# A decoder block in one kernel: attention operands laid out contiguously in DRAM, and the second supertile's SwiGLU operands kept there unsplit

## Chip, cores and metric

The kernel runs on one core of a Trainium2 chip. The metric is the device time of one execution in microseconds; the median of three timed executions before the change is 2718.97 us. The engines are named as in the profile: PE (matrix products), PEld (its weight loads), DVE (vector), ACT (scalar), POOL, and SP, whose queue issues every DMA of this kernel.

## What is computed

One layer on x of 2048 rows by 1024 columns, float32, with one final norm (`h` is RMSNorm(x)):

```
p = h @ W_in                                  # 1024 -> 2560 columns, split among three groups
a = pool_mixer(p[pool cols])                  # trailing means, 64x64 maps, 256 channels
b = diff_attention(p[diff cols])              # 4 heads: (softmax(q1 k1) - lam softmax(q2 k2)) v, causal
c = stick_breaking_attention(p[sb cols])      # 4 heads of 64
x = x + concat(a, b, c) @ W_out
x = x + (silu(h2 @ W_gate) * (h2 @ W_up)) @ W_down     # h2 = RMSNorm(x), 2816 inner columns
out = RMSNorm(x)
```

## The kernel before

All products are made of float32 parts that PE takes at its fast rate: an operand is **split** into a high part (a CAST on ACT, L415) and a low part (a subtraction on DVE, L416), and a product of two split operands is three matmuls (`mm3`, L474, L475, L476).

The program is one list of operations. A planner in the kernel (`Plan.schedule`) gives each operation a cost in ns, lets each engine take, in the order of a priority number, what it believes ready, and issues everything in the order of the planned starts. So every engine, and SP too, runs a fixed row of instructions, each waiting in its place until its inputs are there. The planner believes that a DMA of n bytes takes

```
def dma_ns(nbytes):
    return max(nbytes / 360.0, 450.0)
LAG = {..., "dma": (950.0, 950.0)}
MORE = {"dma": 1080.0, "pe": 0.0}
```

one after the other, and that its data can be read 950 + 1080 ns after that. SBUF is handed out by rings: a ring has some slots, and a new buffer waits until the oldest user of a slot is done.

**First half of the program: projections, attention, output projection.** The sequence is cut into four tiles of 512 rows. `a1_tile` normalizes a tile, multiplies with W_in and stores q, k and v, already split, in DRAM (stores at L611 for q and k, L595 for v). Attention then goes tile by tile over six pairs of heads (four differential, two stick-breaking). For each pair and tile, `load_q` brings q with 64 of its values on the partitions, twice, so that the high and low parts of k can stand under each other: buffer `q0` holds q's high part and `q1` its low part, each by two DMAs of 64 partitions (L626). `load_kv` brings k by two such DMAs (high part to partitions 0 to 63, low part to 64 to 127, L635) and v by one DMA of 128 partitions (L640) or two (L645). `scores` multiplies `q0` (L657) and then `q1` (L658) with k, for 128 query rows `g` at a time; every group of four `g` needs all of `q0` and `q1`. The work of `a1_tile` for the next tile has a lower priority and fills PE between the scores.

**Second half: SwiGLU.** The 2048 rows are two supertiles of 1024. A product of 2x2 blocks is done with seven block products (Strassen-Winograd): operand blocks 11, 21, 22 and sums T1 to T4, each cut in four pieces (`kk`), so 28 split operands. `gate_up` goes over 22 blocks `f` of weights; each takes seven products in four PSUM banks X, Y, W, Z. Some banks hold a partial sum that ACT copies out (L1118) or DVE adds up (L1122) before PE adds the next product to the same bank. The first two and the last two blocks of a supertile are interleaved in pairs.

While the first supertile's blocks run, `head_out` prepares the second supertile's operands in 16 side steps, one per block: eight `rows` steps (load x, norm, transpose on PE, store in `h_d`, L1057) and eight `operands` steps (load four pieces of `h_d`, L1064; four subtractions on POOL, L1070; four splits, L415 and L416; eight stores of the parts in `h1_d`, L1080). `head_in` then loads the 28 split operands (L1098, L1103) as their slots come free at the end of the first supertile. The buffers of the side steps come from a ring `x` of three slots; transposes take banks from the same ring `b` of eight banks as the products.

## Time and profile before

| | |
|---|---|
| timed executions | 2718.97, 2724.35, 2711.99 us |
| median | 2718.97 us |
| profiled execution: its own time | 2719.03 us |
| profiled execution: span from first to last instruction | 2717.2 us |
| PE, DVE, ACT, POOL busy | 96%, 66%, 49%, 32% of the span |
| mean granted TensorE clock | 0.977 |

The busy times are those of instructions in the profile. A matmul there lasts longer than the distance to the next one, since matmuls are pipelined; so idle time of PE is read from its waits and the granted clock, not from the busy share. Attention and the projections fill the span up to about 1383 us. The operand steps of the side work lie between 1576 us (first load at L1064) and 1716 us (last store at L1080); the second supertile's split operands are loaded from 1800 to 1853 us (L1098, L1103), around the change of supertiles; the last sums of gate and up (L1122) are at 2267 us, and the down products follow. The trace leaves the numbers out of names, so `h_d` in it stands for `h_d` and for `h1_d`.

### The profile page before, as it was taken

How to read it: one execution, taken by the hardware profiler on the slowest of the kernel's cores; microseconds unless marked ns; L12 is line 12 of the kernel's file. 1: busy time of each engine (PE TensorE's matmuls, PEld its weight loads, DVE VectorE, ACT ScalarE, POOL GpSimd, SP SyncE). 2: the span in 40 equal slices, each digit the busy share in tenths (PEclk: the TensorE clock that was granted, in tenths of full speed). 3: DMA queues.
4: the chain of work that ended last, by engine and by line, in shares of the span. 5: the costliest groups of instructions: out<-in, count | busy, mean ns of one | idle time of the engine just before them, and what ended most of it. 6: DMA issues, size and time to landing. Idle time of an engine off the chain costs nothing.

```text
span 2717.2 us, 39503 instructions
## 1 busy us (share of the span) xinstructions
PE 2601.9 (96%) x13836; PEld 2176.7 (80%) x13836; DVE 1786.2 (66%) x3131; ACT 1319.3 (49%) x2645; POOL 870.0 (32%) x890
## 2 busy tenths in 40 slices
PE   9989989989999999999989999999999998999998
PEld 7878778877888788888978877888888886888886
DVE  6366787758887888788656666545444447558557
ACT  4365566646666666665534444323333333445444
POOL 1001212212254124133015456535454544132041
PEclk9989999989999999999999999999999999999999
DMA  6786585556564775664534457465222338335223
GB/s 217 245 251 184 160 245 160 155 155 202 153 177 147 225 203 147 192 178 161 166 118 155 155 184 239 158 220 199 101 102 97 109 129 291 118 95 194 93 90 120
DMA packets 223480, 454.27 MB, mean 167 GB/s; under 512 B 23720, under 2 KB 70952, under 8 KB 223280
## 3 DMA queue, kind: packets, MB, share of 16 engines
q1 hardware_dynamic: 223280, 451.75, 52.9%
q8 instruction: 108, 1.77, 0.3%
q14 instruction: 92, 0.75, 0.1%
HBM read 321.11 MB, written 130.55 MB: 166 GB/s over the span
## 4 chain that ended last, share of the span: by engine, by line
PE 72%; DMA 9%; DVE 9%; issue 3%; ACT 2%; POOL 1%; SPq 1%; DVEq 0%; ACTq 0%; POOLq 0%
PE bank L474 16%; PE bank L476 16%; PE bank L475 16%; DVE d L416 4%; DMA d<-q_d 4%; PE bank L657 3%; PE bank L681 3%; PE bank L658 3%; DMA d<-wo_d 2%; PE bank L924 2%; PE bank L923 2%; PE bank L925 2%; ACT d L415 1%; PE bank L562 1%; PE bank L781 1%
## 5 line engine op out<-in xcount | busy, mean ns | idle before, releaser
L474 PE MATMUL bank<-d 128*128 128x512 f32 x2296 | 919.0, 400 | 14.0 <-DVE d L1122 9.8
L476 PE MATMUL bank<-d 128*128 128x512 f32 x2296 | 910.3, 396 | 5.7 <-DVE d L416 5.4
L416 DVE TENSOR_TENSOR d<-d 128x512 fp32r<-128x512 f32 (+2 forms) x672 | 614.6, 938 | 457.5 <-ACT d L415 281.2
L475 PE MATMUL bank<-d 128*128 128x512 f32 x2296 | 909.3, 396 | 3.4 <-DVE d L416 3.4
L415 ACT CAST d<-d 128x512 fp32r<-128x512 f32 (+2 forms) x672 | 489.0, 758 | 651.0 <-PE bank L476 352.3
L961 POOL TENSOR_TENSOR d<-d 128x512 f32<-128x512 f32 x336 | 520.0, 1556 | 846.3 <-DVE d L416 622.9
L474 PEld LDWEIGHTS bank<-d 128*128 128x128 f32 x2296 | 435.7, 190 | 116.0 <-DVE d L1122 12.4
L476 PEld LDWEIGHTS bank<-d 128*128 128x128 f32 x2296 | 434.3, 189 | 110.3 <-DVE d L416 8.7
L475 PEld LDWEIGHTS bank<-d 128*128 128x128 f32 x2296 | 434.8, 189 | 101.3 <-DVE d L416 5.1
L416 DVE TENSOR_TENSOR d<-bank,d 128x512 fp32r<-128x512 f32 (+3 forms) x381 | 219.3, 603 | 139.7 <-ACT d L415 138.7
L819 POOL TENSOR_TENSOR d<-d 128x512 f32<-128x512 f32 (+3 forms) x160 | 160.4, 1003 | 397.9 <-DVE d L815 375.6
L415 ACT CAST d<-bank 128x512 fp32r<-128x512 f32 (+3 forms) x381 | 187.5, 529 | 194.0 <-PE bank L681 122.0
L729 ACT ACTIVATE d<-bank,d 128x512 f32<-128x512 f32 (+3 forms) x320 | 198.9, 627 | 128.4 <-DVE d L726 120.3
L751 POOL TENSOR_SCALAR d<-d 128x512 f32<-128x512 f32 (+3 forms) x144 | 95.8, 681 | 448.7 <-ACT d L741 318.1
L726 DVE TENSOR_REDUCE d<-bank 128x1 f32<-128x512 f32 (+3 forms) x320 | 186.9, 602 | 61.6 <-PE bank L658 31.1
L657 PE MATMUL bank<-d 128*128 128x512 f32 (+3 forms) x480 | 203.7, 425 | 24.8 <-ACT d L729 9.0
L658 PE MATMUL bank<-d 128*128 128x512 f32 (+3 forms) x480 | 181.9, 382 | 25.5 <-DMA d<-q_d 25.5
L1122 DVE TENSOR_TENSOR d<-bank,d 128x512 f32<-128x512 f32 x176 | 121.0, 687 | 116.0 <-PE bank L476 98.7
L815 DVE TENSOR_TENSOR_SCAN d<-d,bank 128x512 f32<-128x512 f32 (+3 forms) x160 | 174.3, 1090 | 19.6 <-ACT d L807 8.1
L1118 ACT COPY d<-bank 128x512 f32<-128x512 f32 x132 | 77.3, 586 | 221.7 <-PE bank L476 196.9
L681 PE MATMUL bank<-ident,d 128*128 128x128 f32 x1088 | 157.5, 279 | 3.4 <-DVE d L772 2.6
L923 PE MATMUL bank<-d 128*128 128x256 f32 x512 | 149.5, 292 | 2.8 <-DMA d<-wo_d 1.1
(133 smaller groups left out, 3593.5 us busy)
## 6 DMA issues: line engine op xcount, KB each, us to landing
d<-in_w_gu_dram SPq DMA_DIRECT2D x88, 512.0 KB, 3.5
d<-in_w_in_dram SPq DMA_DIRECT2D x80, 512.0 KB, 4.6
d<-k_d SPq DMA_DIRECT2D x120, 256.0 KB, 6.6
d<-wo_d SPq DMA_DIRECT2D x52, 512.0 KB, 6.0
d<-q_d SPq DMA_DIRECT2D x96, 256.0 KB, 6.3
d<-vd_d SPq DMA_DIRECT2D x40, 512.0 KB, 4.9
g_d<-d SPq DMA_DIRECT2D x66, 256.0 KB, 2.1
d<-g_d SPq DMA_DIRECT2D x66, 256.0 KB, 2.7
```

Source lines behind the costliest of these rows:

```text
L415: pl.op("act", act_ns(n, psum), lambda: nc.scalar.copy(hi(), src()), r=r, w=[whi], prio=prio)
L416: pl.op("dve", dve_ns(n), lambda: nc.vector.tensor_sub(lo(), src(), f32(hi())), r=[*r, *after, whi], w=[wlo], prio=prio)
L474: nc.tensor.matmul(o, a_hi, b_hi, start=first, stop=False, **kw)
L475: nc.tensor.matmul(o, a_hi, b_lo, start=False, stop=False, **kw)
L476: nc.tensor.matmul(o, a_lo, b_hi, start=False, stop=last, **kw)
L657: nc.tensor.matmul(s.t[:, :n], q[0].t[:, r, qs], kt.t[:, r, :n], start=True, stop=False)
L658: nc.tensor.matmul(s.t[:, :n], q[1].t[:, r, qs], kt.t[:, r, :n], start=False, stop=j < t)
L681: nc.tensor.transpose(tp.t[:, c:c + P], rows[qb][kb // 4].t[:, (kb % 4) * P:(kb % 4 + 1) * P], ident)
L726: pl.op("dve", dve_ns(n), lambda s=s, n=n, mc=mc, sm=sm: nc.vector.tensor_reduce(sm.t[:, mc:mc + 1], s.t[:, :n], AX, ALU.max, negate=True) ...
L729: pl.op("act", act_ns(n, True, 2), lambda s=s, n=n, e=e, mc=mc, lc=lc, sm=sm: nc.scalar.activation(e.t[:, :n], s.t[:, :n], AF.Exp, bias=sm ...
L923: nc.tensor.matmul(o, m[:, 0, cs], wh.t[:, k % 4, :], start=k == 0, stop=False)
L961: pl.op(eng, ns, lambda: en.tensor_tensor(out(), a(), b(), op), r=r, w=w, prio=prio)
```

## The change

Five edits: the tensors in DRAM for q, k, v have one tile per pair and row tile, in the order in which attention reads them; q comes in two halves of 256 query rows (high and low part together), each one DMA whose partitions are the 64 values of q, each one twice; k comes by one DMA, with high and low part on alternating partitions, and v by one DMA; the transposes of the second half have banks 6 and 7 for themselves and the gate and up products banks 0 to 5; and `operands` stores T1 to T4 unsplit (`t_d`), while `head_in` loads them and the pieces of `h_d` and splits them there. The side steps get a rising priority number instead of one for all.

```diff
-    q_d = [dram.tile([2, P, S], F32, name=f"q_d{p}") for p in range(PAIRS)]
-    k_d = [dram.tile([2, P, S], F32, name=f"k_d{p}") for p in range(PAIRS)]
-    vd_d = [dram.tile([P, S // P, 2, P], F32, name=f"vd_d{p}") for p in range(DIFF_PAIRS)]
-    vs_d = [dram.tile([P, S // P, 2, 64], F32, name=f"vs_d{p}") for p in range(2 * SB_PAIRS)]
+    q_d = [[dram.tile([2, 64, 2, 2, 256], F32, name=f"q_d{p}_{t}") for t in range(NT)] for p in range(PAIRS)]
+    k_d = [[dram.tile([64, 2, 2, TQ], F32, name=f"k_d{p}_{t}") for t in range(NT)] for p in range(PAIRS)]
+    v_d = [[dram.tile([P, D], F32, name=f"v_d{p}_{t}") for t in range(NT)] for p in range(PAIRS)]
...
-                    pl.op("dma", dma_ns(P * 4096), lambda st=st, dst=dst[pair]: nc.sync.dma_start(
-                        dst[:, :, t0:t0 + TQ].rearrange("l p t -> p l t"), f32(st.t)),
-                        r=[st], w=[mk[pair][t]], prio=prio)
+                    for r in range(2):
+                        pl.op("dma", dma_ns(P * 2048), lambda st=st, dst=dst[pair][t], r=r, isq=isq: nc.sync.dma_start(
+                            dst[:, :, r].rearrange("h d l t -> d h (l t)") if isq else dst[:, :, r],
+                            f32(st.t[64 * r:64 * r + 64])), r=[st], w=[(mk[pair][t], r)], prio=prio)
...
     def load_q(pl, rg, t, p, prio):
-        q = [rg["q0"].new(), rg["q1"].new()]
-        for hl in range(2):
-            for dup in range(2):
-                pl.op("dma", dma_ns(64 * 4096) * 1.3, lambda hl=hl, dup=dup: nc.sync.dma_start(
-                    f32(q[hl].t[64 * dup:64 * dup + 64]),
-                    q_d[p][hl, :, t * TQ:(t + 1) * TQ].rearrange("(r d) t -> d r t", r=2)),
-                    r=[m_q[p][t]], w=[(q[hl], dup)], prio=prio)
+        q = []
+        for h in range(2):
+            qh = rg["q"].new()
+            q.append(qh)
+            pl.op("dma", dma_ns(P * 4096), lambda h=h, qh=qh: nc.sync.dma_start(
+                f32(qh.t), q_d[p][t][h].rearrange("(d o) r l t -> d o (r l t)", o=1).to_broadcast([64, 2, D])),
+                r=[m_q[p][t]], w=[qh], prio=prio)
...
-        for hl in range(2):
-            pl.op("dma", dma_ns(64 * 4096) * 1.3, lambda hl=hl: nc.sync.dma_start(
-                f32(k.t[64 * hl:64 * hl + 64]),
-                k_d[p][hl, :, j * TQ:(j + 1) * TQ].rearrange("(r d) t -> d r t", r=2)),
-                r=[m_k[p][j]], w=[(k, hl)], prio=prio)
...
+        pl.op("dma", dma_ns(P * 4096), lambda: nc.sync.dma_start(
+            f32(k.t), k_d[p][j].rearrange("d l r t -> (d l) r t")), r=[m_k[p][j]], w=[k], prio=prio)
+        pl.op("dma", dma_ns(P * 4096), lambda: nc.sync.dma_start(f32(v.t), v_d[p][j]), r=[m_v[p][j]], w=[v], prio=prio)
...
-            nc.tensor.matmul(s.t[:, :n], q[0].t[:, r, qs], kt.t[:, r, :n], start=True, stop=False)
-            nc.tensor.matmul(s.t[:, :n], q[1].t[:, r, qs], kt.t[:, r, :n], start=False, stop=j < t)
+            nc.tensor.matmul(s.t[:, :n], qh.t[:, c0:c0 + P], kt.t[:, r, :n], start=True, stop=False)
+            nc.tensor.matmul(s.t[:, :n], qh.t[:, c0 + 256:c0 + 256 + P], kt.t[:, r, :n], start=False, stop=j < t)
...
-                        pt = rg["b"].new()
+                        pt = rg["bt"].new()
...
-                for src, i, n, n0 in ((raw, 1, 2, 0), (raw, 3, 1, 2), (tt, 0, 2, 3), (tt, 2, 2, 5)):
-                    o = rg["x"].new([2, 2, 256], F32R)
-                    flat = lambda v, n=n: v.rearrange("p n t -> p (n t)")
-                    split(pl, lambda o=o, n=n: flat(o.t[:, 0, :n, :]), lambda o=o, n=n: flat(o.t[:, 1, :n, :]),
-                          lambda src=src, i=i, n=n: flat(src.t[:, i:i + n, :]), n * 256, False,
-                          [(src, i + m) for m in range(n)], (o, 0), (o, 1), prio)
-                    for l in range(2):
-                        pl.op("dma", dma_ns(P * 1024 * n), lambda o=o, l=l, n=n, n0=n0: nc.sync.dma_start(
-                            h1_d[kk][:, n0:n0 + n, l, c * 256:(c + 1) * 256], f32(o.t[:, l, :n, :])),
-                            r=[(o, l)], w=[(m_h1[kk], (n0, l, c))], prio=prio)
+                pl.op("dma", dma_ns(P * 4096), lambda: nc.sync.dma_start(
+                    t_d[kk][:, :, c * 256:(c + 1) * 256], tt.t), r=[tt], w=[(m_t[kk], c)], prio=prio)
...
-            return [lambda b=b: rows(b) for b in range(8)] + [
-                lambda kk=kk, c=c: operands(kk, c) for kk in range(4) for c in range(2)]
+            return [lambda b=b: rows(b, prio + b) for b in range(8)] + [
+                lambda kk=kk, c=c: operands(kk, c, prio + 8 + 2 * kk + c) for kk in range(4) for c in range(2)]
...
-                for kk in range(4):
+                for k2 in (0, 2):
+                    raw = rg["x"].new([2, TQ], F32)
+                    if n[0] == "T":
+                        for i in range(2):
+                            load(pl, (raw, i), lambda raw=raw, i=i: raw.t[:, i, :], t_d[k2 + i][:, int(n[1]) - 1, :],
+                                 [m_t[k2 + i]], P * 2048, prio)
                     else:
...
+                        k, c0 = k2 + 4 * (n[0] == "2"), TQ * (n[1] == "2")
+                        load(pl, raw, lambda raw=raw: raw.t, h_d[k:k + 2, :, c0:c0 + TQ].rearrange("k p t -> p k t"),
+                             [m_h], P * 4096, prio)
+                    for i in range(2):
+                        kk = k2 + i
...
+                        split(pl, hi, lo, lambda raw=raw, i=i: raw.t[:, i, :], TQ, False, [(raw, i)], kh, kl, prio)
+                        ops[n][kk] = (hi, lo, kh, kl)
...
-        q0=ring([2, TQ], F32R, ("w", [31, 12])), q1=ring([2, TQ], F32R, ("w", [32, 13])),
+        q=ring([D], F32R, ("w", [31, 32, 12, 13])),
...
-        b=banks(range(8)),
+        b=banks(range(6)), bt=banks((6, 7)),
     )
+    rm["bd"] = banks(range(8))
```

The whole kernel now issues 1264 DMAs instead of 1419. Because the costs and buffers that the planner sees are others, it plans the whole program anew, so the order on every engine changes from the first attention pair on. Three places follow; a name `d_` with a number is a buffer in SBUF, and lines of the changed kernel have other numbers.

SP's row where the q of one pair of the third tile is stored and loaded, before (`L611` is the store, `L626` the loads, `L640` loads of v, `L412` loads of weights, `L707` a store of attention's output):

```order
L611 DMA q_d2_62<-d_6060 128x2x512
L626 DMA d_6113<-q_d2_62 64x2x512
L412 DMA d_6123<-in_w_in_dram 128x1024
L626 DMA d_6113<-q_d2_62 64x2x512
L611 DMA q_d3_63<-d_6118 128x2x512
L412 DMA d_6166<-in_w_in_dram 128x1024
L626 DMA d_6181<-q_d2_62 64x2x512 x2
L640 DMA d_6201<-vd_d2_74 128x1024
L707 DMA o_d2_82<-d_6214 128x512
```

The same place now (`L613` the stores, `L630` the loads of q's halves, `L637` of k, `L639` of v):

```order
L637 DMA d_6054<-k_d2_1_93 128x1024
L613 DMA q_d2_2_70<-d_6076 64x2x512 x2
L630 DMA d_6137<-q_d2_2_70 128x1x1024
L412 DMA d_6153<-in_w_in_dram 128x1024
L630 DMA d_6170<-q_d2_2_70 128x1x1024
L613 DMA q_d3_2_74<-d_6142 64x2x512 x2
L412 DMA d_6199<-in_w_in_dram 128x1024
L639 DMA d_6218<-v_d2_1_117 128x1024
L698 DMA o_d2_134<-d_6258 128x512
```

Four loads of 64 partitions have become two of 128, the first of which is enough for the first scores, and the store has become two of 64 partitions. In the whole row of SP, 14 loads of q or k stand within six places behind the store that they read.

DVE's row at an operand step of the first supertile, before (`L1122` adds a bank to a buffer, `L416` is a split's low part, `L1128` a product):

```order
L416 TENSOR_TENSOR d_17593<-d_17559,d_17593 128x512
L1122 TENSOR_TENSOR d_17599<-bank3_170,d_17599 128x512
L416 TENSOR_TENSOR d_17619<-d_17425,d_17572 128x1024
L416 TENSOR_TENSOR d_17632<-d_17559,d_17632 128x256
L416 TENSOR_TENSOR d_17642<-d_17588,d_17642 128x512
L416 TENSOR_TENSOR d_17664<-d_17588,d_17664 128x512
L416 TENSOR_TENSOR d_17679<-d_17525,d_17621 128x1024
L1122 TENSOR_TENSOR d_17689<-bank7_186,d_17677 128x512
L1122 TENSOR_TENSOR d_17677<-bank5_178,d_17677 128x512
```

The same stretch now:

```order
L1111 TENSOR_TENSOR d_17509<-bank2_218,d_17509 128x512
L416 TENSOR_TENSOR d_17532<-d_17345,d_17487 128x1024
L416 TENSOR_TENSOR d_17592<-d_17443,d_17534 128x1024
L1111 TENSOR_TENSOR d_17599<-bank1_214,d_17590 128x512
L1111 TENSOR_TENSOR d_17590<-bank0_210,d_17590 128x512
```

The four splits of the side step (512, 256, 512, 512 columns) are gone from between the additions of banks, which are now at `L1111`.

ACT's row in the first supertile's last two blocks, before (`L1118` copies a bank, `L1125` is silu, `L415` a split's high part):

```order
L1118 COPY d_18610<-bank0_158 128x512
L1118 COPY d_18631<-bank1_162 128x512
L415 CAST d_18652<-d_18580 128x1024
L1125 ACTIVATE d_18610<-d_18610 128x512
L415 CAST d_18676<-d_18605 128x1024
L1125 ACTIVATE d_18631<-d_18631 128x512
L1118 COPY d_18701<-bank0_158 128x512
L1118 COPY d_18723<-bank1_162 128x512
```

The same place now, with `L1107` for the copies (`d_18477`, `d_18489` and `d_18541` are loads from `h_d` and `t_d`):

```order
L1107 COPY d_18463<-bank4_226 128x512
L415 CAST d_18486<-d_18404 128x1024
L415 CAST d_18513<-d_18477 128x512
L415 CAST d_18534<-d_18477 128x512
L1107 COPY d_18546<-bank3_222 128x512
L415 CAST d_18554<-d_18489 128x512
L415 CAST d_18560<-d_18489 128x512
L415 CAST d_18568<-d_18541 128x512
L1107 COPY d_18575<-bank4_226 128x512
L415 CAST d_18577<-d_18541 128x512
```

The splits that left the side steps now stand between the copies of the last two blocks, and each waits there for its load.

## Rows read from the trace of the kernel before

**Rows 1.** The page, parts 1 and 2: busy time of PE; PE's granted clock.

```profile
PE 2601.9 (96%) x13836; PEld 2176.7 (80%) x13836; DVE 1786.2 (66%) x3131; ACT 1319.3 (49%) x2645; POOL 870.0 (32%) x890
...
PEclk9989999989999999999999999999999999999999
```

**Rows 2.** Windows: length, busy us (instructions) of PE, PEld, DVE, ACT, POOL; PEclk; DMA.

```profile
0.00:1383.00 1383.00, 1298.00 (x8241) 1128.31 (x8241) 1015.43 (x1969) 804.35 (x1801) 325.54 (x526) 0.96 0.63 186
1383.00:1600.00 217.00, 214.93 (x948) 174.28 (x949) 137.06 (x208) 96.44 (x179) 92.86 (x64) 0.98 0.40 138
1600.00:1700.00 100.00, 90.96 (x374) 71.55 (x373) 67.76 (x71) 41.45 (x65) 66.13 (x51) 0.97 0.70 235
1700.00:1800.00 100.00, 99.82 (x431) 80.61 (x430) 50.24 (x57) 35.04 (x51) 47.52 (x33) 1.00 0.38 129
1800.00:1880.00 80.00, 80.00 (x347) 64.87 (x346) 39.62 (x41) 26.47 (x37) 35.53 (x25) 1.00 0.79 286
```

**Rows 3.** PE's waits in the whole span: total us, times, longest us.

```profile
PE bank L658 <- DMA d<-q_d: 25.5, 14, 3.7
PE bank L474 <- DVE d L1122: 9.8, 6, 3.7
PE bank L657 <- ACT d L729: 9.0, 13, 2.8
PE bank L657 <- DMA d<-k_d: 6.5, 3, 3.4
...
PE bank L657 <- DMA d<-q_d: 2.0, 3, 1.3
```

**Rows 4.** Timeline of PE at 576 to 583 us: start, length, instruction, [idle before <- releaser].

```profile
576.30 0.45 PE L657 MATMUL bank<-d 128*128 128x512 f32 x1
...
580.45 0.77 PE L658 MATMUL bank<-d 128*128 128x512 f32 x1 [3.70 <-DMA d<-q_d]
```

**Rows 5.** Timeline of SP's queue at 570 to 590 us.

```profile
571.09 1.24 SPq L626 DMA_DIRECT2D d<-q_d  x2
```

**Rows 6.** The page, part 6: DMA issues, KB each, median us from issue to landing.

```profile
d<-k_d SPq DMA_DIRECT2D x120, 256.0 KB, 6.6
...
d<-q_d SPq DMA_DIRECT2D x96, 256.0 KB, 6.3
d<-vd_d SPq DMA_DIRECT2D x40, 512.0 KB, 4.9
...
q_d<-d SPq DMA_DIRECT2D x24, 512.0 KB, 3.4
k_d<-d SPq DMA_DIRECT2D x24, 512.0 KB, 4.9
```

**Rows 7.** Instructions of L626 and of L640: ns min/median/max that SP is busy.

```profile
L626 SPq DMA_DIRECT2D d<-q_d x96: 573/580/1285, 38.3 to 1149.7; - x96
...
L640 SPq DMA_DIRECT2D d<-vd_d x40: 319/326/1323, 63.3 to 1152.8; - x40
```

**Rows 8.** Waits of SP's queue in the whole span.

```profile
SPq L635 <- DMA k_d<-d: 17.8, 8, 3.6
```

**Rows 9.** Waits of all engines from 1600 to 1700 us.

```profile
ACT d L415 <- DMA h_d<-d: 23.5, 11, 4.7
...
ACT d L415 <- DMA d<-h_d: 19.2, 6, 5.7
...
PE bank L474 <- DVE d L1122: 8.5, 4, 3.7
```

**Rows 10.** Timeline from 1622 to 1632 us.

```profile
1624.60 0.62 ACT L415 CAST d<-d 128x512 fp32r<-128x512 f32 x1 [5.67 <-DMA d<-h_d]
...
1628.54 0.50 PE L474 MATMUL bank<-d 128*128 128x512 f32 x1 [3.73 <-DVE d L1122]
```

**Rows 11.** Groups by form, 1600 to 1720 us: busy, mean ns | idle before.

```profile
L416 DVE TENSOR_TENSOR d<-d 128x512 fp32r<-128x512 f32 x28 | 27.4, 981 | 26.0 <-ACT d L415 26.0
...
L415 ACT CAST d<-d 128x512 fp32r<-128x512 f32 x28 | 17.4, 620 | 43.6 <-DMA d<-h_d 20.8 <-DMA h_d<-d 8.7 <-PE bank L476 8.7
```

More of the change, by code (lines that the diff above doesn't have):

```diff
@@ L310, in hybrid_block_kernel @@
     h_d = dram.tile([KB, P, 2 * TQ], F32, name="h_d")
-    h1_d = [dram.tile([P, 7, 2, TQ], F32, name=f"h1_d{k}") for k in range(4)]
+    t_d = [dram.tile([P, 4, TQ], F32, name=f"t_d{k}") for k in range(4)]
     ident = const.tile([P, P], F32, name="ident")
@@ L399, in hybrid_block_kernel @@
     m_g = [{n: [Buf() for _ in range(NH)] for n in GNAMES} for _ in range(2)]
-    m_h, m_h1 = Buf(), [Buf() for _ in range(4)]
+    m_h, m_t = Buf(), [Buf() for _ in range(4)]
     m_va = [Buf() for _ in range(NT)]
@@ L545, in a1_tile @@
         if t == 0:
-            constants(pl, {"w": rb["q1"], "h": rb["p0"]}, prio + 0.5, xs[3:])
+            constants(pl, {"w": rb["q"], "h": rb["p0"]}, prio + 0.5, xs[3:])
         late = []
@@ L1036, in head_out, with rows @@
         def head_out(prio):
-            def rows(b):
+            def rows(b, prio):
                 xb = rg["x"].new()
@@ L1043, in rows @@
                 for k4 in range(2):
-                    pt = rg["b"].new()
+                    pt = rg["bt"].new()
                     def tr(k4=k4, pt=pt):
@@ L1058, in rows, with operands @@
                     h_d[:, :, b * P:(b + 1) * P].rearrange("k p t -> p k t"), ht.t), r=[ht], w=[(m_h, b)], prio=prio)
-            def operands(kk, c):
+            def operands(kk, c, prio):
                 raw, tt = rg["x"].new([4, 256], F32), rg["x"].new([4, 256], F32)
@@ L1090, in head_in @@
             for n in ("11", "21", "T2", "T1", "T3", "T4", "22"):
[L1091 to L1105 removed]
+                for k2 in (0, 2):
[4 more added lines that the diff above has]
+                                 [m_t[k2 + i]], P * 2048, prio)
+                    else:
+                        k, c0 = k2 + 4 * (n[0] == "2"), TQ * (n[1] == "2")
[3 more added lines that the diff above has]
+                        kk = k2 + i
+                        if spare[0] and n[0] != "T" or n == "T4" and kk == 3 and spare[0]:
+                            spare[0] -= 1
+                            kh, kl = rg["hh"].new(), rg["hl"].new()
+                            hi, lo = (lambda kh=kh: kh.t), (lambda kl=kl: kl.t)
+                        else:
+                            h = rg["hw"].new()
+                            hi, lo, kh, kl = (lambda h=h: h.t[:, 0, :]), (lambda h=h: h.t[:, 1, :]), (h, 0), (h, 1)
+                        split(pl, hi, lo, lambda raw=raw, i=i: raw.t[:, i, :], TQ, False, [(raw, i)], kh, kl, prio)
+                        ops[n][kk] = (hi, lo, kh, kl)
@@ L1317, in down @@
                 four = range(4)
-                new = lambda: [rg["b"].new() for _ in four]
+                new = lambda: [rg["bd"].new() for _ in four]
                 X = new()
```

44 lines of the change are left out of this document (11 added, 33 removed).

## The prediction, made before the changed kernel was run

> **What bounds the kernel now.** I read the page first. PE is busy for 96% of the span, no other engine for more than 66% [rows 1], so a change pays only where it takes away idle time of PE or lets the granted clock stay up. The windows say where that is [rows 2]: up to 1383 us PE is idle for 1383 − 1298 = 85 us, and the mean granted clock is 0.96. [...]
>
> PE's waits name the causes [rows 3]. The largest is L658, the second product of a score, for loads of q: 25.5 us in 14 waits, with 2.0 us more at L657. Loads of k cost 6.5 us. The 9.8 us of L474 behind DVE's L1122 belong to the second half; 8.5 of them lie between 1600 and 1700 us [rows 9]. The long waits of the first half are followed by a slow clock: after the wait at 580.45 us the matmul lasts 0.77 us, where the one before it lasted 0.45 [rows 4].
>
> **Loads of q (edit 1).** At 576.30 us L657 runs, since `q0` has landed, and L658 then stands until 580.45 us for `q1` [rows 4], whose two loads SP issued from 571.09 to 572.33 us [rows 5]. One load of q occupies SP for 0.58 us and lands 6.3 us after its issue (medians) [rows 6, 7]. The fourth one therefore lands 3 × 0.58 + 6.3 = 8.0 us after the first is issued. The planner counts 4 × 0.95 + 2.03 = 5.8 us for it, by the constants in the code, so L658 stands in PE's row 2.2 us too early; the measured waits average 27.5 / 17 = 1.6 us.
> Now the first scores need one load, of 512 KB to 128 partitions. The trace has that shape in the load of v: 0.33 us on SP, 4.9 us to landing [rows 6, 7]. The planner counts 1.46 + 2.03 = 3.5 us, so the products stand 1.4 us too early. Loads that arrive 3.1 us sooner thus give only 0.8 us per wait, because the planner moves the products up by the other 2.3. Scaled, the 27.5 us become 27.5 × 1.4 / 2.2 = 17.5 (saved: 10); taking 0.8 off each of 17 waits saves 14. I take 12. Ends: 0, if PE waits as before, and 27.5.
>
> **Loads of k (edit 2).** By the same reckoning the second half of k landed 0.6 + 6.6 = 7.2 us after the first issue [rows 6], against 3.9 planned; now 4.9 against 3.5. The 6.5 us shrink by (3.3 − 1.4) / 3.3: saved, 4. Ends 0 and 6.5. Loads of v are fewer by 20; no wait of PE for v stands among the rows, so that is worth nothing by itself.
>
> **Stores of q and k (edit 3).** Each of 48 stores becomes two of 64 partitions. The 128-partition store lands after 3.4 (q) to 4.9 us (k) [rows 6]; no row shows a store of 64 partitions. From below, the second half goes out 0.37 us later and lands as the whole did; from above, it takes as long as the 64-partition loads, 6.3 us, so up to 0.4 + 2.9 = 3.3 us more. SP already stood 17.8 us in 8 waits for a k just being stored [rows 8], and everything behind such a wait on SP's queue stands too: weights, v, the next q. In the new order 14 loads follow their store closely. Ends: 14 × 0.4 = 6 and 14 × 3.3 = 46 us. I take 6, since each half carries half of the bytes.
> [...]
>
> **Clock.** In the first half 55 us of clock loss stand beside 85 us of idle time, 0.65 per us. Net idle time saved there is 12 + 4 − 6 = 10 us, so the clock gives back another 6.
>
> **The operand steps (edit 4).** Between 1600 and 1700 us ACT's casts wait 23.5 us for their buffers' stores and 19.2 us for loads of `h_d` [rows 9]. In one case ACT stands 5.67 us for such a load, its cast is late, DVE's subtraction behind it too, and so is L1122, for whose bank PE then waits 3.73 us [rows 10]. The change takes all casts, subtractions and part stores out of these steps; loads, POOL's subtractions and one store stay. What goes is the 9.0 us of idle time in that window and 0.03 × 100 = 3 us of clock [rows 2]: saved, 12 us. The count agrees: 57 matmuls at 100 / 431 = 0.232 us are 13 us. Ends: 0, if POOL's wait for the same loads delays its weight sums instead, and 13.
>
> **Splits at the change of supertiles (edit 5).** The 28 splits now run around 1800 to 1880 us: 28 × 0.98 = 27 us on DVE and 28 × 0.62 = 17 us on ACT [rows 11]. DVE is busy there for 39.6 us of 80 and ACT for 26.5 [rows 2], so 67 and 44 of 80: they fit, and the cover is that idle time. But each now stands in the queue behind a load, and copies of banks stand behind them. Since the last two blocks are interleaved, between a product and the next one in the same bank lie three others, 36 matmuls or 8.4 us at 0.232; waits for a load of the size of [rows 10] fit into that once. I take 2 us. Ends: 0, and 14 loaded pairs of operands at 12 / 8 = 1.5 us (what a side step costs now): 21.
>
> **At nothing:** six banks for the products instead of eight, and graded priorities. A block holds four banks at a time, and from 1383 to 1600 us, with all transposes of the side steps, PE idles for 2 us of 217 [rows 2]. If that cover is gone, transposes and copies stand in PE's way as in the operand steps, some 1 us per step: 8 us.
>
> **Sum,** against the profiled execution's own 2719.0 us (0.1 over the median): −12 − 4 + 6 − 6 − 12 + 2 = −26, that is 2693 us.
>
> **Rivals.**
> *A: the waits for q move to the first product.* PE's row is planned anew, and where q has only just been computed the products move up as far as the loads get faster. For it: 27.5 us in 17 waits look like a planner's error, and that error stays. Then the first half gives nothing, the second −10: 2709.
> *B: the half stores (slower).* Place: SP's queue behind the 14 stores. If a half takes as long to land as the 64-partition loads and most of it reaches PE, say 35 of the 46 us, with 0.65 for the clock 58; less 26 for q and k with their clock, less 10: +22, 2741. It turns the sign when more than 22 of the 46 us reach PE. Against it: before, such waits cost SP 17.8 us and PE less. [...]
> *C: the loads at the change of supertiles take the place of the operand steps.* ACT stands for 14 pairs as it did for eight steps; PE loses 21 us there, and the sum is 2693 + 19 = 2712. Against it: the interleaved blocks.
>
> **Numbers.** Forecast 0.50, A 0.22, B 0.18, C 0.10. A difference below 0.5%, 13.6 us, can hardly be told from none: below 2705.4 is faster, above 2732.6 slower. The forecast's own range is 2668 to 2708: lower if most waits for q go (15 more with their clock), higher if the stores cost 10 more. Faster: 0.9 of the forecast, 0.4 of A, 0.25 of C, together 0.57. Slower: 0.75 of B and a little of A and C, 0.16. Same: 0.27. The range for 8 in 10 goes from 2664, below which the forecast alone could come, to 2736, which takes in A, C and the milder half of B.
>
> **What would show it.** Right: waits at the scores for q and k together below 20 us (34 before); the window of the operand steps with no wait of PE for DVE's sums and a clock of 1.00; no wait above 1 us at the change of supertiles. Wrong: stores of 64 partitions that land after 6 us, and SP's waits for them well above 20 us; the first product of a score waiting as long as the second did; PE waits behind ACT's copies between 1780 and 1880 us; or, outside all steps, attention's other waits (for DVE and ACT) grown by the new order by more than 15 us.

## The result, and the profile after

The changed kernel takes 2688.02 us (median of 4 runs, 2685.21 to 2688.5) against 2720.24 us for the kernel before on the same chip (4 runs, 2711.99 to 2724.35): a ratio of 0.9883, 95% interval 0.9859 to 0.9908, 32 us faster. The profiled execution took 2685.21 us, its span is 2683.3 us. The forecast was 2693.

Lines move by some ten: the first product of a score is L648 (was L657), the second L649 (L658), the loads of q L630, of k L637, the stores of both L613, the copies of SwiGLU's banks L1107 (L1118), their sums L1111 (L1122).

Windows of the kernel after; columns as in [rows 2]. The first row is the whole first half, the next three are parts of it, the last four are stages of the second half:

```profile
0.00:1360.00 1360.00, 1284.15 (x8258) 1112.21 (x8258) 1021.05 (x1986) 817.64 (x1823) 334.63 (x526) 0.97 0.58 191
...
0.00:400.00 400.00, 372.95 (x2248) 313.46 (x2248) 271.38 (x641) 221.59 (x497) 61.91 (x101) 0.98 0.67 223
400.00:800.00 400.00, 382.53 (x2435) 332.39 (x2436) 316.60 (x567) 268.94 (x598) 133.34 (x206) 0.99 0.53 175
...
1080.00:1360.00 280.00, 255.63 (x1843) 231.73 (x1841) 198.68 (x367) 144.98 (x309) 57.23 (x87) 0.93 0.53 176
...
1360.00:1577.00 217.00, 216.96 (x961) 175.99 (x960) 120.88 (x195) 88.33 (x154) 92.26 (x62) 1.00 0.36 123
1577.00:1642.00 65.00, 61.60 (x254) 49.26 (x253) 29.91 (x29) 20.21 (x34) 53.77 (x50) 0.95 0.69 222
1642.00:1770.00 128.00, 128.00 (x554) 103.84 (x553) 61.03 (x68) 44.59 (x63) 63.52 (x42) 1.00 0.33 115
1770.00:1860.00 90.00, 85.39 (x357) 68.18 (x356) 64.03 (x68) 41.09 (x64) 39.85 (x26) 0.96 0.50 169
```

Against the first row of [rows 2]: the first half ends at 1360 us where it ended at 1383. PE idles there for 76 us (85 before), and its busy time for about as many matmuls (8258 and 8241) fell from 1298 to 1284 us, with a mean granted clock of 0.97 for 0.96. So of 23 us, 9 are idle time and 14 are clock.

PE's waits in the whole span, as in [rows 3]:

```profile
PE bank L648 <- ACT d L720: 10.9, 12, 4.0
PE bank L882 <- DVE d L887: 7.9, 2, 7.5
PE bank L648 <- DVE d L806: 6.5, 7, 2.3
PE bank L648 <- DMA d<-k_d: 6.4, 2, 4.7
...
PE bank L474 <- ACT d L1107: 3.9, 2, 3.0
...
PE bank L648 <- DMA d<-q_d: 0.8, 1, 0.8
```

The 27.5 us of waits for q are 0.8. Those for k stand as they were, 6.4 for 6.5. Since idle time as a whole fell by 9 us only, other waits grew: without q and k they were 85 − 34 = 51 us and are 76 − 7 = 69. The growth is in the waits for DVE (all those of the first half together: 24 us before, 42 after); one of 7.5 us at L882 is the longest.

DMA issues of the kernel after (KB, median us to landing), as in [rows 6], and below them SP's waits for data just being stored, as in [rows 8]:

```profile
d<-k_d SPq DMA_DIRECT2D x60, 512.0 KB, 4.8
...
d<-q_d SPq DMA_DIRECT2D x48, 512.0 KB, 4.5
...
q_d<-d SPq DMA_DIRECT2D x48, 256.0 KB, 3.4
k_d<-d SPq DMA_DIRECT2D x48, 256.0 KB, 4.2
```
```profile
SPq L637 <- DMA k_d<-d: 29.3, 10, 4.6
...
SPq L630 <- DMA q_d<-d: 8.2, 3, 2.9
```

A half store of 64 partitions lands no later than the whole one did (3.4 and 4.2 us for 3.4 and 4.9), yet SP stands longer for k: 29.3 us where it stood 17.8 [rows 8].

In the second half two places still cost something. Timeline of the kernel after, some rows of ACT, PE and POOL (times in us; in brackets the idle time before and what ended it) in the operand steps and at the change of supertiles:

```profile
1622.36 0.74 POOL L1061 TENSOR_TENSOR d<-d 128x256 f32<-128x256 f32 x1 [2.60 <-DMA d<-h_d]
...
1628.68 1.04 ACT L415 CAST d<-d 128x1024 fp32r<-128x1024 f32 x1 [8.61 <-POOL d L952]
...
1630.78 0.80 PE L474 MATMUL bank<-d 128*128 128x512 f32 x1 [3.05 <-ACT d L1107]
...
1792.08 6.54 POOL L952 TENSOR_TENSOR d<-d 128x512 f32<-128x512 f32 x4 [20.92 <-DMA d<-in_w_gu_dram]
...
1811.82 1.05 ACT L415 CAST d<-d 128x1024 fp32r<-128x1024 f32 x1 [5.45 <-POOL d L952]
...
1816.28 0.79 PE L476 MATMUL bank<-d 128*128 128x512 f32 x1 [2.63 <-DVE d L416]
```

Read each from the bottom up. At 1630.78 us PE waits for a copy that stands on ACT behind a cast of weights; that cast waited for POOL's weight sums (L952), and these stood behind a subtraction of an operand step that waited for its load of `h_d`. At 1816.28 us the low part of weights is late because their sums on POOL are, and these had no weights: POOL idles 20.92 us for `in_w_gu_dram`. In SP's order those loads now stand behind loads of `t_d`: 13 of these go out from 1771.89 us on, and the next two loads of weights at 1785.65.

### The profile page after: what moved, and what is told of

Read it like the earlier page. It is cut to its first block, busy times and chain, and to the rows that moved or that the text cites. A ratio compares the mean times of both kernels' runs of the same rounds, so it can differ in the third digit from the quotient of the medians.

```text
span 2683.3 us, 39226 instructions
## 1 busy us (share of the span) xinstructions
PE 2582.0 (96%) x13836; PEld 2158.9 (80%) x13836; DVE 1768.1 (66%) x3127; ACT 1323.8 (49%) x2645; POOL 879.9 (33%) x890
## 4 chain that ended last, share of the span: by engine, by line
PE 62%; DVE 9%; DMA 4%; ACT 3%; issue 2%; POOL 2%; SPq 0%; DVEq 0%; POOLq 0%; ACTq 0%
PE bank L476 15%; PE bank L474 15%; PE bank L475 15%; DVE d L416 3%; PE bank L672 3%; PE bank L648 2%; DVE d L806 2%; PE bank L649 2%; PE bank L915 2%; PE bank L914 2%; PE bank L916 2%; DMA d<-wo_d 1%; POOL d L952 1%; PE bank L817 1%; PE bank L816 1%
## 5 line engine op out<-in xcount | busy, mean ns | idle before, releaser
L416 DVE TENSOR_TENSOR d<-d 128x512 fp32r<-128x512 f32 (+1 forms) x668 | 608.8, 934 | 458.4 <-ACT d L415 231.7
L475 PE MATMUL bank<-d 128*128 128x512 f32 x2296 | 906.8, 395 | 3.4 <-DVE d L416 3.4
L952 POOL TENSOR_TENSOR d<-d 128x512 f32<-128x512 f32 x336 | 520.6, 1558 | 870.4 <-DVE d L416 610.2
L415 ACT CAST d<-d 128x512 fp32r<-128x512 f32 (+1 forms) x668 | 489.0, 762 | 611.4 <-PE bank L476 364.7
L475 PEld LDWEIGHTS bank<-d 128*128 128x128 f32 x2296 | 434.2, 189 | 100.8 <-DVE d L416 5.3
L416 DVE TENSOR_TENSOR d<-bank,d 128x512 fp32r<-128x512 f32 (+4 forms) x381 | 220.0, 604 | 113.6 <-ACT d L415 104.8
L415 ACT CAST d<-bank 128x512 fp32r<-128x512 f32 (+4 forms) x381 | 187.7, 527 | 184.7 <-PE bank L672 108.2
L742 POOL TENSOR_SCALAR d<-d 128x512 f32<-128x512 f32 (+3 forms) x144 | 102.8, 730 | 440.5 <-ACT d L732 394.6
L648 PE MATMUL bank<-d 128*128 128x512 f32 (+3 forms) x480 | 199.9, 417 | 28.8 <-ACT d L720 10.9
L1107 ACT COPY d<-bank 128x512 f32<-128x512 f32 x132 | 77.6, 588 | 257.1 <-PE bank L476 231.9
L1111 DVE TENSOR_TENSOR d<-bank,d 128x512 f32<-128x512 f32 x176 | 121.1, 688 | 124.6 <-PE bank L476 117.8
L649 PE MATMUL bank<-d 128*128 128x512 f32 (+3 forms) x480 | 176.7, 371 | 0.0
```

The costliest lines, as they stand in the source:

```text
L415: pl.op("act", act_ns(n, psum), lambda: nc.scalar.copy(hi(), src()), r=r, w=[whi], prio=prio)
L416: pl.op("dve", dve_ns(n), lambda: nc.vector.tensor_sub(lo(), src(), f32(hi())), r=[*r, *after, whi], w=[wlo], prio=prio)
L475: nc.tensor.matmul(o, a_hi, b_lo, start=False, stop=False, **kw)
L648: nc.tensor.matmul(s.t[:, :n], qh.t[:, c0:c0 + P], kt.t[:, r, :n], start=True, stop=False)
L649: nc.tensor.matmul(s.t[:, :n], qh.t[:, c0 + 256:c0 + 256 + P], kt.t[:, r, :n], start=False, stop=j < t)
L952: pl.op(eng, ns, lambda: en.tensor_tensor(out(), a(), b(), op), r=r, w=w, prio=prio)
```

## The experiments

The stages of every kernel, read from its one profiled run: attention (to the first copy of a SwiGLU bank), gate and up (to the last of their sums), down (to the end), in us. "Ratio" is to the kernel before, run on the same chip in turn.

| kernel | attention | gate/up + down | median us | ratio, 95% |
|---|---|---|---|---|
| before | 1382.8 | 884.0 + 450.4 | 2720.24 | |
| after | 1360.1 | 875.8 + 447.4 | 2688.02 | 0.9883 (0.9859 to 0.9908) |
| e1_attn | 1359.6 | 880.4 + 448.3 | 2688.63 | 0.985 (0.9799 to 0.9901) |
| e2_second | 1387.1 | 880.0 + 448.8 | 2720.82 | 0.9978 (0.9952 to 1.0004) |
| e3_halfstores | 1396.5 | 886.4 + 451.0 | 2742.43 | 1.0083 (1.0053 to 1.0113) |
| e4_bothq | 1357.5 | 881.1 + 449.7 | 2687.11 | 0.9847 (0.9804 to 0.9891) |
| e5_planq | 1373.2 | 892.6 + 449.8 | 2719.95 | 0.9968 (0.9948 to 0.9989) |
| e6_subs_dve | 1357.6 | 878.8 + 448.5 | 2686.59 | 0.9857 (0.9828 to 0.9887) |
| e9_planqkv | 1348.5 | 880.1 + 448.7 | 2682.91 | 0.9871 (0.9841 to 0.99) |
| e10_q64 | 1719.5 | 881.3 + 449.0 | 3052.29 | 1.122 (1.1192 to 1.1247) |
| e11_k64 | 1632.2 | 882.2 + 449.9 | 2968.09 | 1.0915 (1.0888 to 1.0941) |
| e12_q64b | 1362.8 | 880.7 + 448.3 | 2698.16 | 0.9901 (0.9866 to 0.9936) |
| e13_wholek | 1355.6 | 875.6 + 448.1 | 2682.89 | 0.9845 (0.9815 to 0.9876) |
| e14_wholek_plan | 1349.7 | 883.0 + 449.0 | 2681.64 | 0.9845 (0.9818 to 0.9872) |

Since every edit has the whole row planned anew, code that an edit does not touch moves too: the second half as it is after spans 1323 to 1332 us over nine kernels, as it was before 1329 to 1342 over four. Differences of a few us between two kernels are not told apart here, and a stage's figure is that of one execution.

**The two halves of the change by themselves.** `e1_attn` joins attention as after with SwiGLU as before, `e2_second` the other way round (no further line is changed).

> The kernel before with the attention edits alone (q, k, v in DRAM, the loads, the alternating query rows); SwiGLU and its banks as before. Theory: the two halves of the change add up, and attention's part is the 22.7 us by which the first copy of SwiGLU came earlier: 2720 - 23 = 2697 us (2693 to 2701), end of attention near 1360 us. Rival: part of the first half's gain came from the new SwiGLU (its first operands are prepared while the output projection runs): then the end of attention lies later than 1365 and the time over 2702.

> The kernel before with the SwiGLU edits alone (own transpose banks, graded steps, operands unsplit in DRAM); attention as before. Theory: 2720 - 11 = 2709 us: 8 us from the operand steps and the change of supertiles, 3 us from the down products. Rival: the 3 us of the down products came with the other order of attention and not with these edits: then 2712; or the second half's gain depends on where attention leaves off: then under 5 us, 2715 or more.

Attention's part alone gives −23 us in its stage (1359.6), as in the full change, and its median (2688.63) is below the range expected and within 1 us of the full change; so it is where nearly all comes from. SwiGLU's part alone gives a ratio of 0.9978, −6 us where 11 were expected, with an interval that just includes no change. By stages: the second half is 1328.7 us long on average in nine kernels that have it as after (all but `e6_subs_dve`) and 1335.7 in four that have it as before, −7.

The first copy of a bank does not come at the same point of PE's work in every kernel. Counting matmuls (13836 in each trace) shows better where time is won. Start of the n-th one, in us:

| kernel | 8600th | 9189th | 9994th | 10384th | last |
|---|---|---|---|---|---|
| before | 1469.3 | 1600.1 | 1800.8 | 1891.5 | 2706.0 |
| after | 1440.0 | 1571.5 | 1763.6 | 1861.7 | 2672.4 |
| e1_attn | 1441.6 | 1572.1 | 1774.5 | 1865.2 | 2677.1 |
| e2_second | 1471.3 | 1603.0 | 1794.9 | 1891.6 | 2705.0 |

The 8600th lies early in gate and up; the operand steps lie between the 9189th and the 9994th, the change of supertiles between the 9994th and the 10384th. The kernel after is 29 us ahead at the 8600th, 37 behind the operand steps, 30 behind the change of supertiles and 34 at the end. Over all kernels (`e6_subs_dve` left out) the stretch of the operand steps takes 200.7 to 204.6 us where SwiGLU is as before (four) and 189.9 to 192.7 where it is as after (nine), 11 less by the means; that of the change of supertiles takes 90.6 to 91.3 and 96.4 to 99.8, 7 more. So the operand steps do gain, and the splits and loads at the change of supertiles give more than half of it back; `e2_second` shows both (−9 and +6).

**What took q's waits away?** In the kernel after a score needs only the half of q that holds its 128 query rows, so the buffer of one half is free half a pair earlier; this is what the expectations call the alternating rows. First each score waits for both halves of q.

```diff
-        pl.op("pe", 2 * mm_ns(n) + (60 if j == t else 0), qk, r=[qh, kt], w=[s], prio=prio)
+        pl.op("pe", 2 * mm_ns(n) + (60 if j == t else 0), qk, r=[*q, kt], w=[s], prio=prio)
```

> The kernel after, but every score waits for both halves of q, and so both halves stay held until the pair's last score; loads, bytes and layouts are unchanged. Theory of buffers: until tile 3 has been projected q has only two slots, so before, a pair's q could not be loaded before the last score of the pair ahead, and the alternating rows free one slot half a pair earlier. Then the waits for q come back here: 12 to 25 us of PE's waits at the scores, and 2700 to 2715 us. Theory of the prediction (the planner's cost for the loads was too small, and the faster, larger loads mend it): the second load goes out 0.5 us after the first where the planner counts 1.46, so nothing waits: 2686 to 2691 us, waits for q under 3 us.

Waits for q stay away, here in PE's waits of that kernel:

```profile
PE bank L648 <- DMA d<-q_d: 2.6, 4, 0.9
```

So the early release of a half, which the theory of buffers was built on, is not needed. Then the kernel before with the truth told to the planner.

```diff
+        o.more = more
...
-                c.ready = max(c.ready, o.end + self.lag(e, c.eng))
+                c.ready = max(c.ready, o.end + self.lag(e, c.eng) + o.more)
...
-                    r=[m_q[p][t]], w=[(q[hl], dup)], prio=prio)
+                    r=[m_q[p][t]], w=[(q[hl], dup)], prio=prio, more=2200.0)
```

> The kernel before, in which the planner counts 2.2 us more from each load of q to its use; the instructions are the same, only their order is planned anew. Theory of the prediction (planner's error): the 27.5 us of waits for q fall under 8 and the time to about 2700 us (2695 to 2707). Theory of buffers: the loads still go out only after the last score of the pair ahead, so PE has to find other work for 8 us each time, which the planner already looked for in 6 us; waits for q fall, others grow: 2712 to 2722 us.

The first three rows are the head of PE's waits in that kernel, the last is what is left for q (the second product of a score is L659 there):

```profile
PE bank L892 <- DVE d L897: 12.5, 6, 9.2
PE bank L475 <- DVE d L1123: 12.1, 7, 3.0
PE bank L658 <- ACT d L730: 9.9, 11, 2.1
...
PE bank L659 <- DMA d<-q_d: 4.1, 5, 1.0
```

The waits for q do fall as the prediction's reasoning says, from 27.5 to 4.1 us, with no load a bit faster. But the ratio is 0.9968, 9 us (3 to 14), where `e4_bothq` beside it gains 42. The time itself lies in the range that the theory of buffers gave, the gain by the ratio between the two ranges. For the 23 us of waits taken away the 8600th matmul starts 7 us sooner (1462.6); waits for DVE at L892 and L475 head the list. So most of the waits that are planned away come back elsewhere; the kernels that gain more all have loads that land sooner.

**The loads' shape.** Two runs brought q, and k, by DMAs of 64 partitions again. The other operand had to follow in the order of its partitions: in `e10_q64` k's two parts, in `e11_k64` q's two copies stand one under the other, still by one DMA. These lines, the first pair of `e10_q64` and the second of `e11_k64`, are what decided:

```diff
-            f32(k.t), k_d[p][j].rearrange("d l r t -> (d l) r t")), r=[m_k[p][j]], w=[k], prio=prio)
+            f32(k.t), k_d[p][j].rearrange("d l r t -> l d r t")), r=[m_k[p][j]], w=[k], prio=prio)
...
-                f32(qh.t), q_d[p][t][h].rearrange("(d o) r l t -> d o (r l t)", o=1).to_broadcast([64, 2, D])),
+                f32(qh.t), q_d[p][t][h].rearrange("(o d) r l t -> o d (r l t)", o=1).to_broadcast([2, 64, D])),
```

> The kernel after, with each half of q brought by two DMAs of 64 partitions as before (four per pair; the planner counts them as before); k stays one DMA, its high and low parts one under the other. Alternating rows stay. Theory of the load's shape (the 128-partition load is what took the waits away, since they stayed away when both halves were held): waits for q back to 15 to 28 us, end of attention 1372 to 1380, 2700 to 2710 us. Rival, two remedies for one fault: the alternating rows load half a pair ahead and hide a slow load too: waits for q under 5 us, 2686 to 2693 us.

> The kernel after, with k brought by two DMAs of 64 partitions as before; q stays one DMA for each half, its two copies one under the other. The prediction counted the larger load of k at 4 us; its waits are 6.4 us after and were 6.5 before. If they are worth 4: waits for k near 10 us, 2692 to 2695. If k's load is no term at all: 2686 to 2690. If the fewer DMAs on SP's queue are what helped attention (60 more here): over 2697.

Neither theory: 3052 and 2968 us. PE's waits of `e10_q64`:

```profile
PE bank L649 <- DMA d<-k_d: 114.9, 13, 17.9
PE bank L649 <- DMA d<-q_d: 54.5, 11, 13.5
```

The load that was meant to stay as it was, the single DMA of the other operand, had become the trouble (last section); what the two were to tell apart they do not tell. `e12_q64b` does what was meant, with k untouched:

```diff
-            pl.op("dma", dma_ns(P * 4096), lambda h=h, qh=qh: nc.sync.dma_start(
-                f32(qh.t), q_d[p][t][h].rearrange("(d o) r l t -> d o (r l t)", o=1).to_broadcast([64, 2, D])),
+            for m in range(2):
+                pl.op("dma", dma_ns(64 * 4096) * 1.3, lambda h=h, qh=qh, m=m: nc.sync.dma_start(
+                    f32(qh.t[64 * m:64 * m + 64]), q_d[p][t][h, 32 * m:32 * m + 32].rearrange(
+                        "(d o) r l t -> d o (r l t)", o=1).to_broadcast([32, 2, D])),
...
```

> The kernel after, with each half of q brought by two DMAs, one for each 64 partitions (32 values of q, each twice), so that one thing alone differs: the load's shape. k is as in the kernel after. This is what the earlier run with two DMAs for q was meant to show; there the single DMA of k had a pattern whose outermost dimension is 2, and that buried the rest. Theory of the load's shape: waits for q back to 10 to 28 us, 2695 to 2710 us. Rival, two remedies for one fault: the alternating rows load half a pair ahead and hide a slow load too: waits for q under 5 us, 2686 to 2693 us.

The median is in the range of the load's shape, the waits for q are in the rival's; by the ratio (27 us under the kernel before) the time is near 2693, the upper end of the rival's range. The rows are from PE's waits and from the DMA issues of that kernel:

```profile
PE bank L650 <- DMA d<-q_d: 4.1, 3, 2.0
```
```profile
d<-q_d SPq DMA_DIRECT2D x96, 256.0 KB, 4.7
```

A load of the old shape, 256 KB to 64 partitions, lands in 4.7 us from the new layout where it took 6.3 from the old one [rows 6]. So the 128 partitions (4.5) add little, and most of the faster landing is likely that of the contiguous rows in DRAM (4 KB after 4 KB, where they were pieces of 2 KB, 8 KB from one value of q to the next); other traffic differs too between these two kernels, so this is not isolated. Of the 10 us by which this kernel is slower than the one after (the intervals of the two overlap), 3.3 are waits for q; the rest lies outside them.

**The half stores.** In the kernel before, each store of q and k as two:

```diff
-                    pl.op("dma", dma_ns(P * 4096), lambda st=st, dst=dst[pair]: nc.sync.dma_start(
-                        dst[:, :, t0:t0 + TQ].rearrange("l p t -> p l t"), f32(st.t)),
-                        r=[st], w=[mk[pair][t]], prio=prio)
+                    for r in range(2):
+                        pl.op("dma", dma_ns(P * 2048), lambda st=st, dst=dst[pair], r=r: nc.sync.dma_start(
+                            dst[:, 64 * r:64 * r + 64, t0:t0 + TQ].rearrange("l p t -> p l t"),
+                            f32(st.t[64 * r:64 * r + 64])), r=[st], w=[(mk[pair][t], r)], prio=prio)
```

> The kernel before, with each store of q and k made as two of 64 partitions (48 stores become 96); all else as before. By the landing times of the changed kernel (3.7 us for a half, 3.6 for the whole) the price is that of the longer issue alone: 0 to +6 us. [...]

By the ratio it is +23 us (14 to 31), well above the range expected, 14 of them in attention; but not by slow landing, and the loads of k wait 19.8 us for their stores, little more than the 17.8 of before [rows 8]. Landing times, the time of SP for one (min/median/max ns), and PE's waits for q in that kernel:

```profile
q_d<-d SPq DMA_DIRECT2D x48, 256.0 KB, 3.8
k_d<-d SPq DMA_DIRECT2D x48, 256.0 KB, 4.3
```
```profile
L612 SPq DMA_DIRECT2D q_d<-d x48: 580/598/1280, 29.2 to 875.3; - x48
L612 SPq DMA_DIRECT2D k_d<-d x48: 580/599/1493, 78.5 to 932.5; - x48
```
```profile
PE bank L659 <- DMA d<-q_d: 31.6, 15, 6.5
...
PE bank L658 <- DMA d<-q_d: 5.6, 6, 1.7
```

The halves land much as the whole did (3.4 and 4.9). What is new is SP's time: two issues of 0.60 us for one of 0.37 (the median of the 48 stores at L611 in the trace of before), 0.83 us × 48 = 40 us more on the queue that all loads stand in. PE's waits for q rise from 27.5 to 37.2 us. `e13_wholek` takes the halves away from k alone in the changed kernel:

```diff
-    k_d = [[dram.tile([64, 2, 2, TQ], F32, name=f"k_d{p}_{t}") for t in range(NT)] for p in range(PAIRS)]
+    k_d = [[dram.tile([2, 64, 2, TQ], F32, name=f"k_d{p}_{t}") for t in range(NT)] for p in range(PAIRS)]
...
+                    if not isq:
+                        pl.op("dma", dma_ns(P * 4096), lambda st=st, dst=dst[pair][t]: nc.sync.dma_start(
+                            dst.rearrange("r d l t -> (r d) l t"), f32(st.t)), r=[st], w=[mk[pair][t]], prio=prio)
...
-            f32(k.t), k_d[p][j].rearrange("d l r t -> (d l) r t")), r=[m_k[p][j]], w=[k], prio=prio)
+            f32(k.t), k_d[p][j].rearrange("r d l t -> (d l) r t")), r=[m_k[p][j]], w=[k], prio=prio)
```

> The kernel after, with the store of k as one DMA of 128 partitions (k in DRAM in an order that one DMA can store and one can load; the load's pieces are 2 KB where they were 4). If the half stores cost the changed kernel what they cost the kernel before (+14 us in attention for 48 stores more), the 24 of k are worth 5 to 10 us: 2678 to 2683, and SP's wait for k just being stored (29 us in 10 waits) falls under 20. If that cost came from the other order there, nothing: 2685 to 2690.

2682.89 us, at the upper end of the first theory's range, and attention 4.5 us shorter; the interval overlaps that of the kernel after. SP's wait for k is hardly less:

```profile
SPq L640 <- DMA k_d<-d: 27.0, 10, 5.3
```

So the longer wait for k in the changed kernel did not come of the half stores. That SP's issuing time is the price fits three pairs of kernels: 40 us more of it in `e3_halfstores`, 28 more in `e12_q64b` (96 loads of q at 0.57 us for 48 at 0.55) and, by estimate, 18 less in `e13_wholek` (24 whole stores at the 0.37 us of before for 48 halves of k at 0.57) go with an 8600th matmul that starts 13 and 8 us later and 4.5 sooner. It is not shown to be the cause, since each of these edits also has the row planned anew, and a new order alone (`e9_planqkv`, below) moves that matmul by 7 us.

**What is left in the operand steps.** The subtractions of L1061 on DVE:

```diff
-                    pl.op("pool", 2.26 * 256 + 68, lambda o=o, p=p, i=i, q=q, j=j: nc.gpsimd.tensor_tensor(
+                    pl.op("dve", dve_ns(256), lambda o=o, p=p, i=i, q=q, j=j: nc.vector.tensor_tensor(
```

> The kernel after, with the 32 subtractions of the operand steps on DVE instead of POOL. Theory: what is left in that window, PE's wait of 3 us for a copy on ACT at 1631 us, comes from POOL, whose weight sums stand behind a subtraction that waits for h_d. Then no wait of PE over 1 us between 1577 and 1642 us, clock 1.00 there, and gate and up 3 to 5 us shorter: 2682 to 2686. Rival: the load of h_d then holds up DVE, which has more behind it (every low part and sum): a wait as long or longer, 2687 to 2693.

By the waits the rival holds, one of 4.4 us for 3.0; the median, 2686.59, lies between the two ranges and is not told apart from the kernel after. Timeline of that kernel, DVE and PE:

```profile
1612.91 2.02 DVE L1061 TENSOR_TENSOR d<-d 128x256 f32<-128x256 f32 x5 [8.42 <-DMA d<-h_d]
...
1616.72 0.80 PE L474 MATMUL bank<-d 128*128 128x512 f32 x1 [4.42 <-DVE d L1111]
```

The low part and the sum of a bank (L1111) stand on DVE right behind the subtractions that waited for `h_d`. So in both kernels the late load holds up the engine that takes them.

**Towards a faster version.** As in `e5_planq`, with 1400 in place of 2200 at the loads of q, k and v of the kernel after; and then that together with `e13_wholek`.

> The kernel after, in which the planner counts 1.4 us more from each load of q, k and v to its use (4.9 us to landing where it counts 3.5). The same instructions in a new order. If what is left of the waits for loads (7.2 us) is the planner's error: 2680 to 2684. If truthful planning only moves the idle time elsewhere, as with the loads of q before: 2684 to 2692.

> The kernel after with both: k stored by one DMA of 128 partitions, and 1.4 us more counted from each load of q, k and v to its use. Each alone gave about 5 us below the kernel after. If each takes away a wait of its own (SP's longer issues; scores planned too early): 2675 to 2680 us. If both gains are no more than another order of the same work, drawn anew: 2680 to 2690 us.

2682.91 and 2681.64 us, the first in the range of the planner's error, the second in that of another order. The waits for loads of q and k fall from 7.2 to 0.6 and 1.9 us. Both have the shortest attention of all (1348.5 and 1349.7), and both have a longer gate and up than the kernel after (880.1 and 883.0). The last is the fastest median here, 6 us under the kernel after; the intervals overlap, so it is not shown to be faster.

## Why the prediction came out right, and where it did not

The time, 2688, lies 5 us under the forecast and in its own range. The causes named are largely right, but that the sum comes so near is in part luck: most terms were wrong in size, and their errors nearly cancelled. By the stages the first half gives −23 for −16 and the second −11 for −10; counted by matmuls it is −29 up to the 8600th and −5 behind it, so the first half gave more than its terms and the second half less.

- **Loads of q, −12.** The waits fell by 26.7 us, near the upper end of 27.5. The failed step is the proportion, "Scaled, the 27.5 us become 27.5 × 1.4 / 2.2". `e4_bothq` shows it: its loads land 5.7 us after issue, the second 0.55 us behind the first, 6.3 where the planner counts 4.9, an error of 1.3 us, and the waits are 2.6 us. An error of 2.2 us cost ten times that. In `e12_q64b` the second load lands 5.3 us after the first is issued where the planner counts 3.9, and the waits are 4.1 us; in `e5_planq`, where the planner counts the whole 8.0, they are 4.1 too. It looks as if PE's row has some slack against the plan and only what exceeds it is waited for; these few points are all that speaks for it. That the waits came of the planner's error is right (`e5_planq`). Neither the early release of a half (`e4_bothq`) nor the 128 partitions (`e12_q64b`) are needed by themselves; all kernels without the waits but `e5_planq` share the contiguous layout. A kernel with that layout and neither of the other two was not run, so it stays open whether the layout alone does it.
- **Loads of k, −4.** Nothing: 6.4 us of waits for 6.5. The same proportion failed here the other way round. `e9_planqkv` shows that what is left is the planner's error: with 1.4 us more counted, 0.6 us of waits remain.
- **Half stores, +6.** Too low. `e3_halfstores` puts them at +14 in attention in the kernel before; the 4.5 us of `e13_wholek` for k's alone are not clear of the spread. The prediction looked for the price in the landing, where there is none (0.6 us of later issue and 4.2 to landing for k, 4.8 in all where the whole took 4.9; 4.0 for 3.4 for q), and counted the later issue per close load only; SP's time, for everything behind, is the likely price, and no run isolates it from the new order. Of the signs named for being wrong, SP's waits well above 20 us did come (29.3), but they stay with whole stores (27.0 in `e13_wholek`). Rival B's mechanism is refuted (a half lands in 3.4 to 4.3 us, under the 6 us named); `e3_halfstores` took 23 us where B counted 58 with the clock. The loads of 64 partitions in [rows 6], from which the upper end of the term has its 6.3 us, come from another layout in DRAM: from the new one such a load lands in 4.7 us (`e12_q64b`).
- **Clock, −6.** The 55 us of clock loss behind it are an estimate, 0.04 × 1383 by the clock of 0.96 in [rows 2]; no run shows such a loss by itself. It gave 14 us (busy time 1298 to 1284) beside 9 us of net idle time, not 0.65 for each. The loss goes with the waits for q in three kernels: from 400 to 800 us the granted clock is 0.96 before, with 27.5 us of them in the whole span, 0.99 in the kernel after, with 0.8, and 0.98 in `e5_planq`, with 4.1. Windows of the kernel before, to be held against the three parts of the first half shown above for the kernel after:

```profile
0.00:400.00 400.00, 371.45 (x2153) 314.56 (x2154) 256.38 (x593) 208.56 (x464) 55.27 (x95) 0.95 0.72 215
400.00:800.00 400.00, 371.55 (x2264) 320.34 (x2263) 300.85 (x573) 247.04 (x571) 112.23 (x177) 0.96 0.57 167
...
1100.00:1383.00 283.00, 266.09 (x1972) 243.04 (x1970) 216.09 (x408) 158.42 (x346) 61.54 (x95) 0.99 0.58 175
```

  At 800 us PE has started 4683 matmuls where it had started 4417, at a clock of 0.98 and 0.99 for 0.95 and 0.96. In the last 280 us the order turns: 0.93 for 0.99, and 24 us idle for 17. Part of what was won is given back at attention's end. `e5_planq`, whose loads are no faster, shows the same turn:

```profile
400.00:800.00 400.00, 379.19 (x2384) 327.49 (x2383) 310.46 (x555) 255.93 (x576) 119.11 (x190) 0.98 0.61 177
...
1100.00:1373.00 273.00, 249.44 (x1821) 230.23 (x1820) 181.91 (x331) 132.78 (x274) 55.24 (x83) 0.94 0.54 166
```

  That the work which used to fill PE there is already done by then is the likely reason; no run isolates it.
- **Other waits** grew by some 18 us, more than the 15 that the prediction named as a sign of being wrong. It is the counterweight to the larger gain on q, and no term of the sum stood for it.
- **Operand steps, −12.** Right: −11 over the kernels, −9 from before to after (the 57 matmuls of the prediction's count are the difference of two windows in [rows 2]). But the window was to have no wait and a clock of 1.00, and it has one of 3.05 us and 0.95: the lower bound, POOL waiting in ACT's place, is true in part.
- **Splits, +2.** Too low: +7, over the kernels and from before to after. In the window from 1770 to 1860 us PE idles for 4.6 us, at a clock of 0.96. Waits of over 1 us do occur, 2.63 us the longest; that one not from the splits' own loads, as rival C had it, but because the loads of weights stand behind these on SP. With the operand steps it makes some −5 by the means, where the prediction had −10.
- **Rival A** fell: the first product waits 0.8 us for q. **C** fell in size: 7 us, not 21.

## What to carry to other kernels

A wait in a row that is planned ahead need not be proportional to the planner's error: here 1.3 us of error cost a tenth of what 2.2 us cost, so measure how late a load is before scaling its waits. Cost a DMA that is split in two by the time of the queue that issues it too, not only by its landing: here two issues took 0.60 us each where one took 0.37, the halves landed in 3.8 and 4.3 us where the whole took 3.4 and 4.9, and the kernel with 48 such splits took 23 us more. A stage whose idle time is filled from a stock of other work may give part of an early gain back at its end, as here; look at its last windows before adding up. To see which stage gains, count the work done as well as the time: here the stage marks put 11 us behind attention, the count 5.

## What was not expected of the hardware

In two runs a load whose pattern has an outermost dimension of 2 took 22.7 and 17.1 us to its last arrival where it took 4.9 and 4.4 (medians). In `e10_q64` the load of k moves the same 512 KB to the same 128 partitions as in the kernel after, with its pattern as 2 × 64 in place of 128. Worked out from the trace's semaphore events (arrivals for one load; us from issue to the last, min/median/max):

```
after    load of k, 60 loads: 16 arrivals; 3.2 / 4.9 / 8.6
e10_q64  load of k, 60 loads:  3 arrivals; 12.5 / 22.7 / 36.0
after    load of q, 48 loads: 16 arrivals; 3.5 / 4.4 / 8.3
e11_k64  load of q, 48 loads:  3 arrivals; 12.8 / 17.1 / 26.4
```

Of the three arrivals in `e10_q64` the first comes 0.95 us after the issue (median), the other two after 22.2 and 22.7. `e10_q64` takes 364 us more than the kernel after and `e11_k64` 280; both also split the other operand's load, which in `e12_q64b` cost about 10. Why such a load makes three arrivals, and why it takes so long, no run shows.
